# Hybrid trunk kernel: the gated branch and the residual stream turned by 16-bit DMA transposes through one joint tile

## Chip, cores and metric

The kernel runs on one core of a Trainium2 chip. The metric is the device time of one execution in microseconds (us), as the median of the runs. Lines are those of the kernel before (L120 is line 120), unless the text says that they are of the changed kernel.

## What is computed

Four layers on a residual stream x of 256 tokens by 2048 channels, all float32. Each layer normalizes x, multiplies it with one wide input projection, runs a mixer (layers 0 and 3: chunked spatial gating, gMLP; layer 1: forgetting attention; layer 2: differential attention) beside a four-head attention to 256 memory tokens, gates the 2048 joined channels and adds an output projection to x:

```python
for i in range(DEPTH):
    h = rms_norm(x, norm_g[i])
    z = h @ w_in
    ...
    mq = rms_norm(mem_q.reshape(B, S, MEM_HEADS, HEAD_DIM), mem_q_norm_g[i])
    mem_out = memory_attention(mq, mk, mv)
    branch = jnp.concatenate([mix_out, mem_out], axis=-1) * jax.nn.silu(gate)
    x = x + branch @ w_out[i]
```

## The kernel before

**Products and slots.** All large products have tokens on the output partitions: two accumulators of 128 tokens by 512 columns (`acc[0]`, `acc[1]`) form a chunk. The weights arrive as 592 pieces of 256 rows by 512 columns, laid out as a 128x1024 tile (`raw`, 512 KB). A piece makes one slot: 12 TensorE matmuls of 512 columns (L186 to L188). Float32 is kept by splitting each operand into two rounded parts, hi and lo: ScalarE copies `raw` to `whi` (L119), VectorE subtracts to `wlo` (L120), and the three products hi\*hi, hi\*lo, lo\*hi are summed. Eight slots make a chunk.

**What sets the order.** The program is written out in order for TensorE, ScalarE, VectorE and SyncE; each engine keeps the order in which Python reaches its instructions. Ahead of each slot `between_slots` (L144) first lets every running task go on to its next `yield` (`tick`), then splits the piece that is three slots ahead (`split_until`, four buffers each for `whi` and `wlo`), then issues the load of a piece seven slots ahead, then runs the functions put on `late`. I call the work that an engine is given ahead of slot n its stage n. So work that a task gives to an engine in one stage stands ahead of that stage's split, and the split of stage n is needed by TensorE three slots later. ScalarE's split waits until TensorE has left slot n - 1, which frees the buffer.

**Turned tiles.** The next product contracts over channels, so results with tokens on partitions must be turned to have channels there. Three tasks do this:

- `norm_task` (L357) for queries and keys: it normalizes an accumulator (`qn`, L350), separates the upper and lower 16-bit halves of each tile on ScalarE (`pl`, L373), has SyncE issue a DMA transpose of the 16-bit tile (`tt`, L375), and one slot later does the same for the second 128 tokens. Three slots after that VectorE puts the halves together (`qt_t`, L382), ScalarE scales them into `qt`, `kt`, `mqt` or `mkt` (L386), and in the same stage `done()` sets the flag that starts the attention.
- `gate_task` (L632), 16 times: silu of the gate's accumulator (`sg`), times the mixer's output (`br`, L644); then in each of the next two slots TensorE transposes four 128x128 blocks into PSUM (L653), from which `bh` (L657, L659) and `bl` (L663, L665) are made, the operand of the output projection.
- `residual_task` (L813), 12 times with a turn (layers 0 to 2, four chunks each): the new x (`xn`, L827), its store, its squares (L836, put on `late`), and in each of the next two slots four TensorE transposes (L846) and a split into `xh` and `xl` (L221, L222), the operand of the next layer's input projection.

The output projection takes its operand parts in the order 0, 1, 2, 3, 6, 7, 4, 5 in its first chunk (L93), because parts 4 and 5 come from the last gate.

**Memory attention.** `memory` (L870) spawns the memory query's `norm_task` and an `attention_task` (L575) that waits for its flag. That task has 8 units, one per slot: scores of unit n on TensorE (L501), exponential on ScalarE (L509), transposes of the probabilities two slots on (L602), their product with the values three slots on (L593).

Of the kernel before, what the change touches and what calls it, by code (L numbers as in the profile page):

```python
# [20 lines left out]
P = 128  # L21
# [3 lines left out]
KT = D // P  # L25
# [18 lines left out]
def trunk_kernel(  # L44
# [251 lines left out]
    def token_rms(src, r):  # L296
        ss = small.tile([P, 2, 4], F32, tag="ss", name="ss", bufs=2)
        rows = {}
        for n in range(6):
            if n >= 2:  # L300
                for t, row in enumerate(rows.pop(n - 2)):
                    nc.scalar.activation(
                        row, row, AF.Square, accum_out=ss[:, t, n - 2 : n - 1]
                    )
            if n < 4:
                rows[n] = []
                for t in range(2):
                    row = tmp.tile([P, CW], F32, tag="tb", name="row", bufs=4)
                    nc.sync.dma_start(
                        row, src[t * P : (t + 1) * P, n * CW : (n + 1) * CW]  # L310
                    )
                    rows[n].append(row)
            if n < 5:
                yield
        late.append(lambda: finish_rms(ss, r))

    def square_rows(src, rcols):
        sqs = []
        for t in range(2):
            sq = tmp.tile([P, CW], F32, tag="sq", name="sq", bufs=2)  # L320
            if rcols is None:
                nc.scalar.activation(sq, src[t], AF.Square)
            else:
                nc.scalar.activation(sq, src[t], AF.Square, scale=rcols[:, t : t + 1])
            sqs.append(sq)
        return sqs
# [21 lines left out]
    def times_cols(dst, src, cols, n):  # L348
# [5 lines left out]
            ALU.mult,  # L354
        )

    def norm_task(acc, rcols, gain, width, dst, done=None):  # L357
        sqs = square_rows(acc, rcols)
        sc = []
        late.append(lambda: sc.extend(norm_factors(sqs, rcols, width)))  # L360
        yield
        yield
        yield
        qn = []
        for t in range(2):
            q = tmp.tile([P, CW], F32, tag="tb", name="qn", bufs=4)
            times_cols(q, acc[t], sc[t], CW // width)
            qn.append(q)
        turned = []
        for t in range(2):  # L370
            pl = tmp.tile([P, 2, CW], U16, tag="pl", name="pl", bufs=2)
            halves = qn[t].bitcast(U16).rearrange("p (e h) -> p h e", h=2)
            nc.scalar.copy(pl, halves)  # L373
            tt = tmp.tile([P, 8, P], U16, tag="tt", name="tt", bufs=2)
            nc.sync.dma_start_transpose(tt, pl.rearrange("p h e -> p (h e)"))  # L375
            turned.append(tt)
            yield
        yield
        yield
        for t in range(2):  # L380
            qt = tmp.tile([P, CW], F32, tag="tb", name="qt_t", bufs=4)
            nc.vector.tensor_copy(  # L382
                qt.bitcast(U16).rearrange("p (c r h) -> p h c r", c=4, h=2),
                turned[t].rearrange("p (h c) r -> p h c r", h=2),
            )
            nc.scalar.activation(  # L386
                dst[:, :, t * P : (t + 1) * P], qt.rearrange("p (c r) -> p c r", c=4),
                AF.Copy, scale=gain,
            )
        if done:  # L390
            done()

# [70 lines left out]

    def diff_setup():
        ls = small.tile([P, 8], F32, tag="sc", name="lsum")
        pr = tmp.tile([P, CW], F32, tag="sq", name="pr", bufs=2)
# [11 lines left out]
        wrow = tmp.tile([P, CW], F32, tag="sq", name="wrow", bufs=2)  # L478
# [153 lines left out]
    def gate_task(acc, rcols, mos, c, dst, pscale):  # L632
        sgs = []
        for t in range(2):
            sg = tmp.tile([P, CW], F32, tag="ta", name="sg", bufs=2)
            nc.scalar.activation(sg, acc[t], AF.Silu, scale=rcols[:, t : t + 1])
            sgs.append(sg)
        yield
        while mos[c] is None:
            yield  # L640
        br = []
        for t in range(2):
            b = tmp.tile([P, CW], F32, tag="tb", name="br", bufs=4)
            nc.vector.tensor_mul(b, mos[c][t], sgs[t])  # L644
            br.append(b)
        for j in range(2):
            yield
            kp = 2 * c + j
            tb = ps_t.tile([P, 4, P], F32, tag="t", name="tb")
            for kk in range(2):  # L650
                for t in range(2):
                    f = (2 * j + kk) * P
                    nc.tensor.transpose(tb[:, 2 * kk + t, :], br[t][:, f : f + P], ident)  # L653
            tbf = tb.rearrange("p a b -> p (a b)")
            hi, lo = new_parts("b", kp)
            if pscale is None:
                nc.scalar.copy(hi, tbf)  # L657
            else:
                nc.scalar.activation(hi, tbf, AF.Copy, scale=pscale)  # L659

            def rest(hi=hi, lo=lo, tbf=tbf):
                if pscale is None:
                    nc.vector.tensor_sub(lo, tbf, hi.bitcast(F32))  # L663
                else:
                    nc.vector.scalar_tensor_tensor(  # L665
                        lo, tbf, pscale, hi.bitcast(F32), ALU.mult, ALU.subtract
                    )

            late.append(rest)
            dst[kp] = (hi, lo)  # L670


    def gmlp_norm_task(vs, j, flag):
# [139 lines left out]
    def residual_task(acc, i, n, xo, ss, r_next):  # L813
        last = i == DEPTH - 1
        xn = []
        for t in range(2):
            rows, cols = slice(t * P, (t + 1) * P), slice(n * CW, (n + 1) * CW)
            xt = tmp.tile([P, CW], F32, tag="tb", name="xn", bufs=4)
            if last:
                for a in (0, CW // 2):  # L820
                    w = slice(a, a + CW // 2)
                    nc.vector.tensor_add(xt[:, w], acc[t][:, w], xo[t][:, w])
                    (nc.sync, nc.scalar)[a > 0].dma_start(
                        out[rows, cols.start + w.start : cols.start + w.stop], xt[:, w]
                    )
                continue
            nc.vector.tensor_add(xt, acc[t], xo[t])  # L827
            nc.gpsimd.dma_start(x_d[i][n][t], xt)  # L828
            xn.append(xt)
        if last:  # L830
            return

        def squares():
            for t in range(2):
                sq = tmp.tile([P, CW], F32, tag="sq", name="sq", bufs=2)
                nc.scalar.activation(sq, xn[t], AF.Square, accum_out=ss[:, t, n : n + 1])  # L836

        late.append(squares)
        for jj in range(2):
            yield  # L840
            kp = 2 * n + jj
            tb = ps_t.tile([P, 4, P], F32, tag="t", name="tb")
            for kk in range(2):
                for t in range(2):
                    f = (2 * jj + kk) * P
                    nc.tensor.transpose(tb[:, 2 * kk + t, :], xn[t][:, f : f + P], ident)  # L846
            hi, lo = new_parts("x", kp)
            scaled_split(hi, lo, tb.rearrange("p a b -> p (a b)"), KT * (i + 1) + 2 * kp)
            xparts[kp] = (hi, lo)
        if n == 3:  # L850
            finish_rms(ss, r_next)

# [210 lines left out]
```

## Time and profile before

| | |
|---|---|
| median of 3 runs | 1774.13 us (1773.99 to 1775.26) |
| profiled execution, its own time | 1775.19 us |
| its span, first to last instruction | 1773.2 us |
| busy: TensorE matmul, weight load | 1756.5 us, 1445.6 us |
| busy: VectorE, ScalarE, GpSimd | 1045.2 us, 938.6 us, 115.6 us |
| mean granted TensorE clock | 0.999 |
| moved by DMA | 364.38 MB, mean 205 GB/s |

The profiled execution is 1.06 us above the median, and 2.0 us of it lie outside its span. Busy times of TensorE come from pipelined matmuls and overlap, so the distance from one matmul's start to the next one's says more than a busy share. In a timeline row the first two numbers are the start and the length in us; x4 at its end means four instructions merged; a bracket tells the engine's idle time just before it and what ended it.

### The profile page before, as it was taken

What the parts mean: (1) busy time and instruction counts of PE and PEld (TensorE: products, weight loads), DVE (VectorE), ACT (ScalarE), POOL (GpSimd) and SP (SyncE); (2) the same over time, 40 slices, a digit from 0 to 9 for tenths busy, and PEclk for the clock granted to TensorE, in tenths of its full rate; (3) what the DMA queues carried; (4) which work ended last, traced back from release to release, by engine and by line L of the source; (5) the groups of instructions that cost most, each with busy time, mean ns of one, the idle gap of its engine ahead of it and who ended that gap; (6) DMA issues with size and microseconds to landing.
All of it is one profiled execution on the core that took longest, in us unless ns stands there. A gap on an engine that the chain in (4) does not pass through costs nothing.

```text
span 1773.2 us, 22090 instructions
## 1 busy us (share of the span) xinstructions
PE 1756.5 (99%) x8142; PEld 1445.6 (82%) x8142; DVE 1045.2 (59%) x1479; ACT 938.6 (53%) x1313; POOL 115.6 (7%) x138
## 2 busy tenths in 40 slices
PE   9999999999999999999999999999999999999999
PEld 6788887888888878888888887878788888788887
DVE  5655667555555656656555566766665556655553
ACT  5656645544555655556445555665654554554532
POOL 1110101000001001011000110102000000100000
PEclk9999999999999999999999999999999999999999
DMA  8878865555676566566866656645546666545564
GB/s 295 291 240 279 267 229 166 179 183 184 224 232 203 177 209 185 171 201 186 207 224 230 210 179 199 185 163 190 187 159 224 231 218 221 178 165 179 190 219 161
DMA packets 146843, 364.38 MB, mean 205 GB/s; under 512 B 54396, under 2 KB 56756, under 8 KB 146608
## 3 DMA queue, kind: packets, MB, share of 16 engines
q1 hardware_dynamic: 140016, 343.33, 59.9%
q0 software_dynamic: 5280, 18.44, 3.3%
q8 instruction: 64, 1.05, 0.2%
q10 hardware_dynamic: 1440, 1.22, 0.2%
q14 instruction: 43, 0.35, 0.1%
HBM read 339.55 MB, written 12.89 MB: 199 GB/s over the span
## 4 chain that ended last, share of the span: by engine, by line
PE 92%; DMA 3%; issue 2%; ACT 2%; DVE 1%; POOL 0%; SPq 0%; ACTq 0%; DVEq 0%; POOLq 0%
PE acc L186 29%; PE acc L188 28%; PE acc L187 28%; PE tb L593 2%; PE tb L602 1%; PE tb L653 1%; DMA xraw<-in_mem_t_dram 1%; PE s L543 1%; PE s L501 1%; PE sv L719 1%; DMA tt<-pl 1%; PE tb L846 1%; ACT whi L119 1%; DMA bias<-cum_d 1%; DMA row<-in_mem_dram 0%
## 5 line engine op out<-in xcount | busy, mean ns | idle before, releaser
L120 DVE TENSOR_TENSOR wlo<-raw,whi 128x1024 fp32r<-128x1024 f32 x591 | 722.0, 1225 | 569.9 <-ACT whi L119 563.5
L119 ACT CAST whi<-raw 128x1024 fp32r<-128x1024 f32 x591 | 619.3, 1050 | 477.4 <-PE acc L188 400.6
L186 PE MATMUL acc<-whi,xh 128*128 128x512 f32 x1600 | 640.3, 400 | 0.0
L188 PE MATMUL acc<-whi,xl 128*128 128x512 f32 x1600 | 624.8, 390 | 0.0
L187 PE MATMUL acc<-wlo,xh 128*128 128x512 f32 x1600 | 624.2, 390 | 0.0
L186 PEld LDWEIGHTS acc<-whi,xh 128*128 128x128 f32 x1600 | 301.0, 188 | 66.3 <-issue 3.5
L188 PEld LDWEIGHTS acc<-whi,xl 128*128 128x128 f32 x1600 | 300.5, 188 | 64.2
L187 PEld LDWEIGHTS acc<-wlo,xh 128*128 128x128 f32 x1600 | 301.2, 188 | 59.0 <-DVE wlo L120 0.2
L186 PE MATMUL acc<-whi,bh 128*128 128x512 f32 x764 | 300.0, 393 | 0.7 <-ACT bh L221 0.4
L187 PE MATMUL acc<-wlo,bh 128*128 128x512 f32 x764 | 298.1, 390 | 1.2 <-DVE wlo L120 0.9
L188 PE MATMUL acc<-whi,bl 128*128 128x512 f32 x764 | 297.9, 390 | 0.2 <-DVE bl L222 0.2
L187 PEld LDWEIGHTS acc<-wlo,bh 128*128 128x128 f32 x764 | 143.5, 188 | 32.3 <-DVE wlo L120 2.9
L188 PEld LDWEIGHTS acc<-whi,bl 128*128 128x128 f32 x764 | 143.4, 188 | 30.7 <-DVE bl L222 0.5
L186 PEld LDWEIGHTS acc<-whi,bh 128*128 128x128 f32 x764 | 143.5, 188 | 30.6 <-ACT bh L221 0.8
L336 POOL TENSOR_TENSOR sc<-sc,expo 128x8 f32<-128x8 f32 (+1 forms) x23 | 56.6, 2460 | 512.6 <-DVE sc L335 450.3
L606 ACT COPY pt<-tb 128x256 f32<-128x256 f32 (+1 forms) x80 | 27.2, 339 | 114.0 <-PE tb L602 113.9
L373 ACT COPY pl<-qn 128x1024 uint16<-128x1024 uint16 x40 | 41.8, 1044 | 44.8 <-DVE qn L350 42.7
L657 ACT CAST bh<-tb 128x512 fp32r<-128x512 f32 x26 | 15.3, 587 | 48.0 <-PE tb L653 48.0
L222 DVE SCALAR_TENSOR_TENSOR xl<-tb,gk,xh 128x256 fp32r<-128x256 f32 x48 | 23.2, 484 | 29.4 <-ACT xh L221 29.3
L221 ACT ACTIVATE xh<-tb,gk 128x256 fp32r<-128x256 f32 x48 | 22.8, 475 | 32.8 <-PE tb L846 19.5
L828 POOL DMA_DIRECT2D x_d<-xn x24 | 13.2, 549 | 311.9 <-DVE xn L827 311.1
L506 DVE TENSOR_REDUCE st<-s 128x1 f32<-128x256 f32 x32 | 13.5, 421 | 31.5 <-PE s L501 31.5
(167 smaller groups left out, 972.6 us busy)
## 6 DMA issues: line engine op xcount, KB each, us to landing
raw<-in_w_a_dram SPq DMA_DIRECT2D x176, 512.0 KB, 3.3
raw<-in_w_o_dram SPq DMA_DIRECT2D x128, 512.0 KB, 3.9
raw<-in_w_b_dram SPq DMA_DIRECT2D x112, 512.0 KB, 3.5
raw<-in_w_c_dram SPq DMA_DIRECT2D x112, 512.0 KB, 3.3
raw<-in_w_kv_dram SPq DMA_DIRECT2D x63, 512.0 KB, 4.9
x_d<-xn POOLq DMA_DIRECT2D x24, 256.0 KB, 6.3
xo<-x_d SPq DMA_DIRECT2D x24, 256.0 KB, 5.5
lnp<-in_ln_dram SPq DMA_DIRECT2D x12, 256.0 KB, 5.6
```

Source lines behind the costliest of these rows:

```text
L119: nc.scalar.copy(hi, raw)
L120: nc.vector.tensor_sub(lo, raw, hi.bitcast(F32))
L186: nc.tensor.matmul(acc[t], xh[:, c], wh, start=begin, stop=False)
L187: nc.tensor.matmul(acc[t], xh[:, c], wl, start=False, stop=False)
L188: nc.tensor.matmul(acc[t], xl[:, c], wh, start=False, stop=end)
L221: nc.scalar.activation(hi, src, AF.Copy, scale=g)
L222: nc.vector.scalar_tensor_tensor(lo, src, g, hi.bitcast(F32), ALU.mult, ALU.subtract)
L336: nc.gpsimd.tensor_tensor(sc[:, :, :n], sc[:, :, :n], expo.rearrange("p (a b) -> p a b", a=2)[:, :, :n], ALU.pow,)
L373: nc.scalar.copy(pl, halves)
L501: nc.tensor.matmul(s[:, :S], qt[:, h, t * P : (t + 1) * P], mk[:, h * S : (h + 1) * S], start=True, stop=True,)
L593: nc.tensor.matmul(av, pt[:, j * P : (j + 1) * P], vv[:, j, f], start=(j == 0), stop=(j == tiles(t) - 1),)
L606: nc.scalar.copy(pt[:, : nk * P], tb[:, : nk * P])
```

## The change

Two helpers are new. `turn` separates the 16-bit halves of a 128x512 tile on ScalarE and has SyncE issue the DMA transpose; `join` puts two turned tiles (both token halves) together on VectorE into one tile `wide` (128 x 4 x 2 x 128, a single buffer). All three tasks now use them: both halves are turned in one stage, and joined two stages later. `gate_task` and `residual_task` no longer use TensorE; their hi and lo parts are made from `wide` in SBUF. The gate multiplies in place into the mixer's output tile. In `norm_task` one activation over the joint tile takes the place of two, and one more `yield` stands between it and `done()`. Buffers: `pl` now shares the tag of `sq` (3 buffers instead of 2), `tb` has 3 instead of 4, and the rows of `token_rms` move to the tag `mo`.

```diff
+    def turn(src):
+        pl = tmp.tile([P, CW], F32, tag="sq", name="pl", bufs=3).bitcast(U16)
+        nc.scalar.copy(
+            pl.rearrange("p (h e) -> p h e", h=2),
+            src.bitcast(U16).rearrange("p (e h) -> p h e", h=2),
+        )
+        tt = tmp.tile([P, 8, P], U16, tag="tt", name="tt", bufs=2)
+        nc.sync.dma_start_transpose(tt, pl)
+        return tt
+
+    def join(wide, tts):
+        for t in range(2):
+            nc.vector.tensor_copy(
+                wide[:, :, t, :].bitcast(U16).rearrange("p c (r h) -> p h c r", h=2),
+                tts[t].rearrange("p (h c) r -> p h c r", h=2),
+            )
+
+    def new_wide():
+        return tmp.tile([P, 4, 2, P], F32, tag="tw", name="wide", bufs=1)
...
     def norm_task(acc, rcols, gain, width, dst, done=None):
...
+        tts = [turn(q) for q in qn]
+        yield
+        yield
+        wide = new_wide()
+        join(wide, tts)
+        nc.scalar.activation(
+            dst.rearrange("p c (t r) -> p c t r", t=2), wide, AF.Copy, scale=gain
+        )
+        yield
         if done:
             done()
...
     def gate_task(acc, rcols, mos, c, dst, pscale):
...
-            nc.vector.tensor_mul(b, mos[c][t], sgs[t])
-            br.append(b)
+            nc.vector.tensor_mul(mos[c][t], mos[c][t], sgs[t])
+            tts.append(turn(mos[c][t]))
+        yield
+        yield
+        wide = new_wide()
+        join(wide, tts)
         for j in range(2):
-            yield
+            src = wide[:, 2 * j : 2 * j + 2].rearrange("p a b r -> p (a b r)")
             kp = 2 * c + j
-            tb = ps_t.tile([P, 4, P], F32, tag="t", name="tb")
-            for kk in range(2):
-                for t in range(2):
-                    f = (2 * j + kk) * P
-                    nc.tensor.transpose(tb[:, 2 * kk + t, :], br[t][:, f : f + P], ident)
...
             dst[kp] = (hi, lo)
+            yield
...
     def residual_task(acc, i, n, xo, ss, r_next):
...
         late.append(squares)
+        tts = [turn(xt) for xt in xn]
+        yield
+        yield
+        wide = new_wide()
+        join(wide, tts)
         for jj in range(2):
-            yield
             kp = 2 * n + jj
-            tb = ps_t.tile([P, 4, P], F32, tag="t", name="tb")
-            for kk in range(2):
-                for t in range(2):
-                    f = (2 * jj + kk) * P
-                    nc.tensor.transpose(tb[:, 2 * kk + t, :], xn[t][:, f : f + P], ident)
...
             xparts[kp] = (hi, lo)
+            yield
```

**ScalarE, layer 0, around the first chunk of the new x.** `pl` is the tile of separated halves, `sq` the squares, `xh` the hi part of the new operand. Before:

```order
L119 CAST whi<-raw 128x1024 x6
L836 ACTIVATE sq,ss<-xn 128x512 x2
L221 ACTIVATE xh_3895<-tb,gk 128x256 x2
L119 CAST whi<-raw 128x1024
L221 ACTIVATE xh_3924<-tb,gk 128x256 x2
L119 CAST whi<-raw 128x1024 x7
```

Now (lines of the changed kernel):

```order
L360 COPY pl<-xn 128x1024 x2
L119 CAST whi<-raw 128x1024
L843 ACTIVATE sq,ss<-xn 128x512 x2
L119 CAST whi<-raw 128x1024
L221 ACTIVATE xh_3905<-wide,gk 128x256 x2
L119 CAST whi<-raw 128x1024
L221 ACTIVATE xh_3929<-wide,gk 128x256 x2
L119 CAST whi<-raw 128x1024 x5
```

Two copies stand ahead of the split of the chunk's first stage, and the first `xh` comes two stages after them instead of one.

**VectorE, layer 1, the memory query's norm.** `wlo` is the split of a stage, `qt_t` and `wide` the joining of turned halves, `st<-s` the first look at the attention's scores. Before:

```order
L350 TENSOR_TENSOR qn<-acc_4412,sc 128x512
L350 TENSOR_TENSOR qn<-acc_4413,sc 128x512
L120 TENSOR_TENSOR wlo<-raw,whi 128x1024 x4
L382 COPY qt_t<-tt 128x2x512 x2
L506 TENSOR_REDUCE st<-s 128x1
```

Now:

```order
L350 TENSOR_TENSOR qn<-acc_4409,sc 128x512
L350 TENSOR_TENSOR qn<-acc_4410,sc 128x512
L120 TENSOR_TENSOR wlo<-raw,whi 128x1024 x2
L370 COPY wide<-tt 128x2x4x128 x2
L120 TENSOR_TENSOR wlo<-raw,whi 128x1024
L515 TENSOR_REDUCE st<-s 128x1
```

The joining stands two splits after `qn` instead of four, and the scores one split after the joining; against `qn`, the scores come one stage earlier than before.

**SyncE, the first keys of the start, one piece of the difference.** `raw` are the loads of weight pieces.

```order
-L375 DMA_TRANSPOSE tt<-pl 128x8x128
-L106 DMA raw<-in_w_kv_dram 128x1024
-L375 DMA_TRANSPOSE tt<-pl 128x8x128
-L106 DMA raw<-in_w_kv_dram 128x1024 x15
-L375 DMA_TRANSPOSE tt<-pl 128x8x128
-L106 DMA raw<-in_w_kv_dram 128x1024
-L375 DMA_TRANSPOSE tt<-pl 128x8x128
-L106 DMA raw<-in_w_kv_dram 128x1024 x4
+L365 DMA_TRANSPOSE tt<-pl 128x8x128 x2
+L106 DMA raw<-in_w_kv_dram 128x1024 x16
+L365 DMA_TRANSPOSE tt<-pl 128x8x128 x2
+L106 DMA raw<-in_w_kv_dram 128x1024 x5
```

The two transposes of a pair are now issued back to back, ahead of the load of their stage.

## Rows read from the trace of the kernel before

**Rows 1.** The page: busy time and share of TensorE, and its granted clock in 40 slices.

```profile
PE 1756.5 (99%) x8142; PEld 1445.6 (82%) x8142; DVE 1045.2 (59%) x1479; ACT 938.6 (53%) x1313; POOL 115.6 (7%) x138
...
PEclk9999999999999999999999999999999999999999
```

**Rows 2.** The page: the chain that ended last, shares of the span by engine.

```profile
PE 92%; DMA 3%; issue 2%; ACT 2%; DVE 1%; POOL 0%; SPq 0%; ACTq 0%; DVEq 0%; POOLq 0%
```

**Rows 3.** Timeline of TensorE, output projection of layer 0, 495 to 505 us.

```profile
495.26 0.39 PE L188 MATMUL acc<-whi,bl 128*128 128x512 f32 x1
...
495.49 0.60 PE L846 MATMUL tb<-ident,xn 128*128 128x128 f32 x4
...
497.09 0.39 PE L188 MATMUL acc<-whi,bl 128*128 128x512 f32 x1
...
501.67 0.39 PE L188 MATMUL acc<-whi,bl 128*128 128x512 f32 x1
...
503.03 0.39 PE L188 MATMUL acc<-whi,bl 128*128 128x512 f32 x1
```

**Rows 4.** Groups by line: busy us, mean ns of one | idle before, releaser.

```profile
L120 DVE TENSOR_TENSOR wlo<-raw,whi 128x1024 fp32r<-128x1024 f32 x591 | 722.0, 1225 | 569.9 <-ACT whi L119 563.5 <-DMA xraw<-in_mem_t_dram 2.6 <-DMA row<-in_x_dram 2.5
L119 ACT CAST whi<-raw 128x1024 fp32r<-128x1024 f32 x591 | 619.3, 1050 | 477.4 <-PE acc L188 400.6 <-issue 33.2 <-ACT whi L119 9.4
L373 ACT COPY pl<-qn 128x1024 uint16<-128x1024 uint16 x40 | 41.8, 1044 | 44.8 <-DVE qn L350 42.7 <-DMA raw<-in_w_b_dram 2.1
L382 DVE COPY qt_t<-tt 128x1024 uint16<-128x1024 uint16 x40 | 28.0, 744 | 1.9 <-DMA tt<-pl 1.9
L221 ACT ACTIVATE xh<-tb,gk 128x256 fp32r<-128x256 f32 x48 | 22.8, 475 | 32.8 <-PE tb L846 19.5 <-DVE xl L222 13.3
L653 PE MATMUL tb<-ident,br 128*128 128x128 f32 x128 | 19.3, 273 | 0.0
L846 PE MATMUL tb<-ident,xn 128*128 128x128 f32 x96 | 14.4, 272 | 0.0
```

**Rows 5.** The tile `tt`: its issues (ns min/median/max), and time to landing.

```profile
L375 SPq DMA_TRANSPOSE tt<-pl x40: 1237/1237/1331, 65.5 to 1521.3; - x40
...
DMA to landing us min/median/max: 2.7/4.3/6.9
```

**Rows 6.** Waits of TensorE: us in total, times, longest us.

```profile
PE s L501 <- ACT mqt L386: 4.6, 4, 1.2
PE sv L719 <- ACT p L509: 3.9, 2, 2.3
```

**Rows 7.** Timelines of ScalarE, VectorE, TensorE: memory query's norm, layer 0, 266 to 312 us.

```profile
281.37 1.05 ACT L373 COPY pl<-qn 128x1024 uint16<-128x1024 uint16 x1 [3.72 <-DVE qn L350]
...
284.54 0.54 DVE L695 TENSOR_SCALAR v<-v,mv 128x512 f32<-128x512 f32 x1
...
285.85 0.69 DVE L699 TENSOR_TENSOR v<-v,lnp 128x512 f32<-128x512 f32 x1
...
291.40 0.70 PE L501 MATMUL s<-mk,mqt 128*128 128x256 f32 x2 [1.24 <-ACT mqt L386]
```

**Rows 8.** Timelines of SyncE's queue and TensorE: the same norm in layer 1.

```profile
570.76 1.25 SPq L375 DMA_TRANSPOSE tt<-pl  x1
...
581.25 0.70 PE L501 MATMUL s<-mk,mqt 128*128 128x256 f32 x2 [1.13 <-ACT mqt L386]
```

**Rows 9.** Timelines of VectorE and ScalarE: first new x of layer 0, 468 to 500 us.

```profile
469.78 1.28 DVE L827 TENSOR_TENSOR xn<-acc,xo 128x512 f32<-128x512 f32 x2
...
470.27 1.06 ACT L119 CAST whi<-raw 128x1024 fp32r<-128x1024 f32 x1 [1.67 <-PE acc L188]
...
471.22 0.63 ACT L836 ACTIVATE sq<-xn 128x512 f32<-128x512 f32 x1
```

**Rows 10.** Busy time by stretch: us, engines' busy us (instructions), granted clock, DMA share, GB/s.

```profile
301.60:305.00 3.40, 3.40 (x12) 2.82 (x11) 2.33 (x6) 0.98 (x3) 0.00 (x0) 0.50 0.54 180
```

**Rows 11.** The page: what DMA moved in the whole span.

```profile
DMA packets 146843, 364.38 MB, mean 205 GB/s; under 512 B 54396, under 2 KB 56756, under 8 KB 146608
```

More of the change, by code (lines that the diff above doesn't have):

```diff
@@ L307, in token_rms @@
                 for t in range(2):
-                    row = tmp.tile([P, CW], F32, tag="tb", name="row", bufs=4)
+                    row = tmp.tile([P, CW], F32, tag="mo", name="row", bufs=6)
                     nc.sync.dma_start(
@@ L319, in square_rows @@
         for t in range(2):
-            sq = tmp.tile([P, CW], F32, tag="sq", name="sq", bufs=2)
+            sq = tmp.tile([P, CW], F32, tag="sq", name="sq", bufs=3)
             if rcols is None:
@@ L365, in norm_task @@
         for t in range(2):
-            q = tmp.tile([P, CW], F32, tag="tb", name="qn", bufs=4)
+            q = tmp.tile([P, CW], F32, tag="tb", name="qn", bufs=3)
             times_cols(q, acc[t], sc[t], CW // width)
             qn.append(q)
-        turned = []
-        for t in range(2):
[L371 to L376, printed above, removed]
-            yield
+        tts = [turn(q) for q in qn]
         yield
         yield
-        for t in range(2):
[L381 to L389, printed above, removed]
+        wide = new_wide()
[4 more added lines that the diff above has]
+        yield
         if done:
@@ L465, in diff_setup @@
         ls = small.tile([P, 8], F32, tag="sc", name="lsum")
-        pr = tmp.tile([P, CW], F32, tag="sq", name="pr", bufs=2)
+        pr = tmp.tile([P, CW], F32, tag="sq", name="pr", bufs=3)
         for m in range(2):
@@ L477, in diff_setup @@
         nc.tensor.matmul(pb[:NH, :384], rel, onehot, start=True, stop=True)
-        wrow = tmp.tile([P, CW], F32, tag="sq", name="wrow", bufs=2)
+        wrow = tmp.tile([P, CW], F32, tag="sq", name="wrow", bufs=3)
         nc.vector.tensor_copy(wrow[:NH, :384], pb[:NH, :384])
@@ L640, in gate_task, with rest @@
             yield
-        br = []
+        tts = []
         for t in range(2):
-            b = tmp.tile([P, CW], F32, tag="tb", name="br", bufs=4)
-            nc.vector.tensor_mul(b, mos[c][t], sgs[t])
-            br.append(b)
+            nc.vector.tensor_mul(mos[c][t], mos[c][t], sgs[t])
[4 more added lines that the diff above has]
+        join(wide, tts)
         for j in range(2):
-            yield
+            src = wide[:, 2 * j : 2 * j + 2].rearrange("p a b r -> p (a b r)")
             kp = 2 * c + j
-            tb = ps_t.tile([P, 4, P], F32, tag="t", name="tb")
-            for kk in range(2):
-                for t in range(2):
-                    f = (2 * j + kk) * P
-                    nc.tensor.transpose(tb[:, 2 * kk + t, :], br[t][:, f : f + P], ident)
-            tbf = tb.rearrange("p a b -> p (a b)")
             hi, lo = new_parts("b", kp)
             if pscale is None:
-                nc.scalar.copy(hi, tbf)
+                nc.scalar.copy(hi, src)
             else:
-                nc.scalar.activation(hi, tbf, AF.Copy, scale=pscale)
-            def rest(hi=hi, lo=lo, tbf=tbf):
+                nc.scalar.activation(hi, src, AF.Copy, scale=pscale)
+            def rest(hi=hi, lo=lo, src=src):
                 if pscale is None:
-                    nc.vector.tensor_sub(lo, tbf, hi.bitcast(F32))
+                    nc.vector.tensor_sub(lo, src, hi.bitcast(F32))
                 else:
                     nc.vector.scalar_tensor_tensor(
-                        lo, tbf, pscale, hi.bitcast(F32), ALU.mult, ALU.subtract
+                        lo, src, pscale, hi.bitcast(F32), ALU.mult, ALU.subtract
                     )
@@ L817, in residual_task @@
             rows, cols = slice(t * P, (t + 1) * P), slice(n * CW, (n + 1) * CW)
-            xt = tmp.tile([P, CW], F32, tag="tb", name="xn", bufs=4)
+            xt = tmp.tile([P, CW], F32, tag="tb", name="xn", bufs=3)
             if last:
@@ L834, in squares @@
             for t in range(2):
-                sq = tmp.tile([P, CW], F32, tag="sq", name="sq", bufs=2)
+                sq = tmp.tile([P, CW], F32, tag="sq", name="sq", bufs=3)
                 nc.scalar.activation(sq, xn[t], AF.Square, accum_out=ss[:, t, n : n + 1])
         late.append(squares)
-        for jj in range(2):
-            yield
-            kp = 2 * n + jj
-            tb = ps_t.tile([P, 4, P], F32, tag="t", name="tb")
-            for kk in range(2):
-                for t in range(2):
-                    f = (2 * jj + kk) * P
-                    nc.tensor.transpose(tb[:, 2 * kk + t, :], xn[t][:, f : f + P], ident)
-            hi, lo = new_parts("x", kp)
-            scaled_split(hi, lo, tb.rearrange("p a b -> p (a b)"), KT * (i + 1) + 2 * kp)
-            xparts[kp] = (hi, lo)
+        tts = [turn(xt) for xt in xn]
[3 more added lines that the diff above has]
+        join(wide, tts)
+        for jj in range(2):
+            kp = 2 * n + jj
+            hi, lo = new_parts("x", kp)
+            scaled_split(
+                hi, lo, wide[:, 2 * jj : 2 * jj + 2].rearrange("p a b r -> p (a b r)"),
+                KT * (i + 1) + 2 * kp,
+            )
+            xparts[kp] = (hi, lo)
+            yield
         if n == 3:
```

## The prediction

> **What bounds the kernel now.** I read the page first, for which engine is full and at which clock: TensorE is busy 99% of the span, at full clock in every slice, VectorE 59% and ScalarE 53% [rows 1]. Then the chain that ended last: 92% of it is TensorE [rows 2]. So almost every instruction that leaves TensorE's queue shortens the span, and the other engines matter only where TensorE waits for them. Third, TensorE's timeline, for what a transpose really costs there. From 501.67 to 503.03 us six matmuls start in 1.36 us, 0.227 us each; a slot of twelve is 2.72 us. From 495.26 to 497.09 there are also six steps, with four transposes among them, and they take 1.83 us. Four transposes cost 0.47 us [rows 3]. Fourth, TensorE's waits: the list is short. Its largest entries are 4.6 us for the memory query `mqt` (once per layer) and 3.9 us for an exponential in the two gMLP layers [rows 6].
>
> **What is removed.** 16 gates and 12 residual chunks, each with two groups of four transposes: 56 groups, the 128 and 96 transposes of [rows 4]. 56 x 0.47 = **26.3 us**. Lower bound: the merged row of four is 0.60 us long and one is 0.27, so starts lie (0.60 - 0.27) / 3 = 0.11 us apart, 0.44 for four [rows 3, 4], 24.6 us in all. A row's own length, 273 ns, is no price, since the next one starts after 0.11 us. The Trainium skill (TensorE: Matmul & The Clock Gate, Part 4: PE-mode transpose) gives about 275 ns for a 128x128 transpose inside a kernel, at two bytes; the row's length agrees. Priced so, 224 transposes would be 61.6 us and the forecast some 35 us lower; the distance of the starts decides against it.
>
> **What is added off TensorE.** 56 tiles (16 x 2 and 12 x 2) are turned as `norm_task`'s 40 are today. Each costs ScalarE a copy of 1.04 us and VectorE a joining of 0.74 us [rows 4]: 58 us on an engine idle for 835 us, 42 us on one idle for 728 [rows 1]. In `norm_task` one activation replaces two, so ScalarE gains a little. The hi and lo parts are as many as before. The tiles are 256 KB: 56 x 0.26 = 14.7 MB on 364 MB [rows 11], 4% more traffic. SyncE gets 56 issues of 1.24 us [rows 5]; queued behind them are the loads of weight pieces, issued four slots before their split, so about 2.5 us of delay is covered.
>
> **Does the supply of weights hold?** The pair is now joined two stages after it was turned, and VectorE and ScalarE stop there if it has not landed. I follow the first residual chunk [rows 9]. The adds begin at 469.78 and take 0.64 each; the copies run 470.4 to 472.5; the split of that stage 473.5; squares to 474.9; the next split on ScalarE 475.9, on VectorE 477.1 (1.05 and 1.22 [rows 4]). The first transpose is issued at 471.5, the second 1.24 later, at 472.7. It lands L later; today's 40 took 2.7 to 6.9 us, median 4.3 [rows 5]. Behind the landing come a joining (0.74), two `xh` (0.95), the stage's split on ScalarE (1.05) and on VectorE (1.22): 476.7 + L. TensorE needs that split in the fifth slot after 470.25, at 484.1 with its first lo product. So TensorE is served as long as **L is under 7.4 us**. At L = 5 the margin is 2.4 us, at the largest L of today 0.5. A gate's chain is of the same kind (one cast for the two `xh`); its parts 4 and 5 are first read six and seven slots after the gate's product, and are made in stages 3 and 4. The new x has its parts 6 and 7 in stages 2 and 3 and is read in slots 6 and 7. I put the cost at nothing; the cover is the three slots of split weights.
>
> **The memory query.** Here TensorE does stand behind the turned tile. Counted from the end of its product, the query was turned in stages 3 and 4, joined in 7 and read by TensorE in slot 7. Now: turned in 3, joined in 5, read in slot 6. The extra `yield` gives a stage, but the scores also come one slot sooner.
> - Layer 0 [rows 7]: copies 281.37 to 283.5, second issue 283.7, split 284.5 and 285.75, then the gMLP norm's three operations (1.92 us), split to 288.9, joinings 289.65 and 290.4, one activation (about 1.1, as the 1024-element copy of [rows 4] takes 1.04): `mqt` at 291.5, or 292.5 at L = 6.9. Slot 7's scores were due at 291.40 - 1.24 = 290.16, so slot 6's at 287.44. Wait 4.1 to 5.1 us. Layer 3 has the same order of work: the same.
> - Layer 1 [rows 8]: issues 570.76 and 572.0; the second lands at 576.3 (L = 4.3) to 578.9; VectorE is free at 575.3. `mqt` at 578.2 to 580.8, wanted at 581.25 - 1.13 - 2.72 = 577.4. Wait 0.8 to 3.4 us; I take 1.3 (L a little above today's median, since two share the engines). Layer 2 likewise.
>
> Together 10.8 us (9.8 to 17.0) for 4.6 today: **+6.2 us** (+5.2 to +12.4). That the flag is set "later" saves nothing by itself.
>
> **Next waits.** The gMLP layers' 3.9 us [rows 6] come from ScalarE's table loads piling up behind a late `mqt`. With TensorE held one slot earlier the exponentials regain some of that: I take **-2.5 us** (0 to -3.9). Behind the wait in layer 0 the granted clock was 0.50, the lower of its two levels (1.2 of 2.4 GHz), for 3.4 us [rows 10], a loss of 1.7; it may go, or come in layer 3 too: 0 (-1.7 to +1.7). In layers 1 and 2 the memory attention still runs when the next query is joined, and ScalarE's stop there delays a copy of probabilities by up to 2 us, twice: **+1 us** (0 to +4).
>
> **Sum.** -26.3 + 6.2 - 2.5 + 0 + 1 = -21.6. The profiled execution took 1775.19 us and would take 1753.6; it was 1.06 above the median of the runs, so I say **1752.5 us**. With all bounds one way: -26.7 (1747.4) and -6.5 (1767.6).
>
> **Rivals.**
> 1. *The turned tiles come too late: slower.* If two transposes issued back to back take L over 7.4 us in the output projection, beside the loads of the old and the stores of the new x, TensorE runs out of split weights in each of the 28 gate and residual pairs: 1752.5 + 28 x (L - 7.4). Break-even lies at L = 8.2; slower by over 0.2% from L = 8.3; at L = 9 it is 1797 us. For it: the largest of today's is 6.9, and each had the queue to itself. Against it: the median is 4.3 and the whole change is 4% of traffic. The Trainium skill (VectorE: DVE Perf Modes, The three transpose paths and Rules for kernel authors) says to use TensorE where a PSUM destination will do, with 390 ns for a 128x128 two-byte block there and 1309 ns by DMA. Eight such blocks in a row, as one tile has, would be an estimate of 10.5 us and this rival; the trace lands a whole tile in 4.3, so I hold to the row.
> 2. *The gain is handed back by halves.* L between 7.6 and 8.2 on average, or joinings that cost twice 0.74 us through their new access pattern: 1758 to 1775, typically 1769.
> 3. *The query's wait vanishes.* If VectorE reached the joining earlier than I think, all of 4.6, 3.9 and 1.7 us would go: 1775.2 - 26.3 - 10.2 - 1.1 = 1738. Against it: in layer 0 VectorE's own queue holds the joining until 288.9, after slot 6 is due, whatever L is.
>
> That the change might not do what it says I leave out: in the program's order all 56 groups are gone.
>
> **How the numbers follow.** A measurement of this kernel tells a change from none at about 0.2%, 3.5 us. Forecast 0.75 (1747.4 to 1767.6, all of it faster). Rival 1: 0.10 (0.07 slower, 0.03 same). Rival 2: 0.09 (0.04 faster, 0.05 same). Rival 3: 0.06, faster. So faster 0.85, same 0.08, slower 0.07. The range 1745 to 1768 holds the forecast's bounds and leaves out rival 1, half of rival 2 and rival 3, 0.2 in all.
>
> **What would show it.** In the changed profile TensorE's queue should hold transposes of probabilities alone, and matmuls of a residual chunk should start 0.227 us apart throughout. `tt` should show 96 landings with a median of 4 to 6 us; over 7.4 is rival 1, with waits of TensorE for `wlo` or `whi` after a joining. The waits for `mqt` should be about 4 us in layers 0 and 3 and 1 to 2 us in 1 and 2; near zero would be rival 3. If the time falls by 26 us or more with those waits present, the price of a transpose was too low; if transposes are gone and the time stays, look for the new waits in the output projections.

## The result, and the profile after

The changed kernel takes **1757.74 us** (median of 4 runs, 1757.08 to 1759.51) where the kernel before took 1774.16 (4 runs). The ratio is 0.9908 with a 95% interval of 0.9891 to 0.9925: 16.4 us faster, inside the range, where 21.6 were forecast. A later run (run 5 below) whose instructions stood in exactly the same order on every engine gave 0.9892 (0.9877 to 0.9907), so a difference of 2 us between two runs below is not told by the time alone; the waits in the traces tell more.

The profiled execution took 1757.08 us, 18.1 less than that of before. The page of the changed kernel, beside [rows 1] and [rows 11]:

```profile
PE 1736.1 (99%) x7918; PEld 1428.6 (81%) x7918; DVE 1073.9 (61%) x1535; ACT 982.7 (56%) x1349; POOL 122.3 (7%) x138
...
PEclk9999999999999999999999999999999999999999
...
DMA packets 205980, 379.06 MB, mean 216 GB/s; under 512 B 113532, under 2 KB 115892, under 8 KB 205744
...
L370 DVE COPY wide<-tt 128x1024 uint16<-128x1024 uint16 x96 | 68.8, 747 | 20.1 <-DMA tt<-pl 19.5
```

TensorE has 224 instructions fewer (8142 to 7918) and is still full; 14.7 MB more move, as counted ahead. A joining takes 0.747 us (0.744 before). New is the idle time in the last row: VectorE stands 19.5 us for tiles that have not landed (1.9 in [rows 4]).

TensorE's waits, the whole span, beside [rows 6]; then the memory query's wait alone in stretches of layers 0, 1, 2 and 3:

```profile
PE s L510 <- ACT mqt L395: 7.3, 4, 3.7
PE acc L186 <- ACT whi L119: 3.1, 2, 2.8
PE acc L187 <- DVE wlo L120: 2.3, 3, 0.8
...
PE s L510 <- ACT mqt L395: 3.7, 1, 3.7
...
PE s L510 <- ACT mqt L395: 0.2, 1, 0.2
...
PE s L510 <- ACT mqt L395: 0.2, 1, 0.2
...
PE s L510 <- ACT mqt L395: 3.3, 1, 3.3
```

Three things are to be seen. `mqt` costs 7.3 us where 4.6 stood, all but 0.4 of it in layers 0 and 3. The wait of `sv` for an exponential (3.9) is gone. And TensorE now waits for split weights, 5.4 us in all (`wlo` 0.9 before). That last one the prediction had put at nothing.

The granted clock, in stretches that answer to [rows 10] (columns as there):

```profile
290.30:294.00 3.70, 3.23 (x8) 2.56 (x9) 2.31 (x3) 3.67 (x5) 0.00 (x0) 0.54 0.26 66
...
853.70:857.20 3.50, 3.50 (x10) 2.74 (x9) 3.47 (x4) 1.35 (x3) 0.00 (x0) 0.51 0.79 263
...
1509.10:1515.90 6.80, 5.58 (x13) 4.43 (x14) 2.85 (x4) 4.88 (x6) 0.00 (x0) 0.50 0.49 158
```

Three stretches lie near the lower of the two levels (0.50 is 1.2 of 2.4 GHz) where there was one, each behind a standstill of TensorE: for `mqt`, for split weights, for `mqt` again. In 0.5 and 1.2 us of the first and the third TensorE still stood for `mqt`, which the waits count already. What the clock costs is the busy time times what is missing: 3.23 x 0.46 + 3.50 x 0.49 + 5.58 x 0.50 = 6.0 us, against 1.7 before.

The turned tile, beside [rows 5]:

```profile
L365 SPq DMA_TRANSPOSE tt<-pl x96: 1232/1293/8426, 65.6 to 1669.9; - x96
...
DMA to landing us min/median/max: 2.7/3.6/11.0
```

The median landing is shorter than before (3.6 for 4.3; 4 to 6 were forecast). But one issue held SyncE's queue 8.4 us, and one landing took 11.0, far over the 7.4 that the prediction allowed. They belong to one pair, the issue to its second transpose and the landing to its first. It is the first gate of layer 1 (timelines of GpSimd, SyncE's queue, VectorE and TensorE):

```profile
828.41 4.42 POOL L505 DMA_DIRECT2D bias<-bias_d  x8 [39.53 <-DVE lg L532]
...
837.04 9.87 SPq L365 DMA_TRANSPOSE tt<-pl  x2
...
848.05 0.75 DVE L370 COPY wide<-tt 128x1024 uint16<-128x1024 uint16 x1 [6.49 <-DMA tt<-pl]
848.96 0.74 DVE L370 COPY wide<-tt 128x1024 uint16<-128x1024 uint16 x1 [0.16 <-DMA tt<-pl]
...
851.35 0.50 PE L186 MATMUL acc<-whi,xh 128*128 128x512 f32 x1 [2.75 <-ACT whi L119]
852.61 0.51 PE L187 MATMUL acc<-wlo,xh 128*128 128x512 f32 x1 [0.76 <-DVE wlo L120]
```

GpSimd has started to load layer 2's bias at 828.41, as soon as layer 1's attention had read the old one. Two transposes are issued into that transfer: 9.87 us for both instead of some 2.6. VectorE stands 6.49 us at the joining, and TensorE 2.75 + 0.76 = 3.5 us behind it. The prediction's sum counts L from the second issue. That one ended at 846.91 and took 8.43, so it began at 838.48; its tile was there at 848.96, so L is 10.5 and the sum gives 10.5 - 7.4 = 3.1, 0.4 less than measured.

The other 1.9 us of weight waits lie in layer 2. ScalarE's timeline, the first key there:

```profile
1126.91 1.05 ACT L360 COPY pl<-qn 128x1024 uint16<-128x1024 uint16 x1 [0.89 <-DVE qn L350]
1131.83 1.05 ACT L360 COPY pl<-qn 128x1024 uint16<-128x1024 uint16 x1 [3.88 <-DMA tt<-pl]
```

The second rearranging copy waits 3.88 us for the landing of the first transpose. `pl` took over the tag of `sq`, with three buffers for four users here (two squares of the differential attention, two `pl`), so it gets the buffer that this transpose is still reading.

### The profile page after: what moved, and what is told of

It is laid out like the page before. It is cut to its first block, busy times and chain, and to the rows that moved or that the text cites. A ratio compares the mean times of both kernels' runs of the same rounds, so it can differ in the third digit from the quotient of the medians.

```text
span 1755.3 us, 21797 instructions
## 1 busy us (share of the span) xinstructions
PE 1736.1 (99%) x7918; PEld 1428.6 (81%) x7918; DVE 1073.9 (61%) x1535; ACT 982.7 (56%) x1349; POOL 122.3 (7%) x138
## 4 chain that ended last, share of the span: by engine, by line
PE 91%; DVE 3%; DMA 3%; ACT 2%; issue 1%; SPq 0%; ACTq 0%; DVEq 0%
PE acc L186 29%; PE acc L187 28%; PE acc L188 28%; PE tb L602 2%; DVE wlo L120 1%; DMA xraw<-in_mem_t_dram 1%; DMA tt<-pl 1%; PE s L510 1%; ACT whi L119 1%; PE tb L611 1%; PE s L552 1%; PE sv L726 1%; DVE wide L370 0%; PE s L527 0%; DMA raw<-in_w_kv_dram 0%
## 5 line engine op out<-in xcount | busy, mean ns | idle before, releaser
L119 ACT CAST whi<-raw 128x1024 fp32r<-128x1024 f32 x591 | 612.7, 1048 | 332.1 <-PE acc L188 239.9
L370 DVE COPY wide<-tt 128x1024 uint16<-128x1024 uint16 x96 | 68.8, 747 | 20.1 <-DMA tt<-pl 19.5
L221 ACT ACTIVATE xh<-wide,gk 128x256 fp32r<-128x256 f32 x48 | 21.8, 501 | 44.0 <-DVE wide L370 44.0
L360 ACT COPY pl<-mo 128x1024 uint16<-128x1024 uint16 x32 | 31.9, 1043 | 23.8 <-DVE mo L652 23.8
L663 ACT CAST bh<-wide 128x512 fp32r<-128x512 f32 x26 | 16.1, 617 | 44.0 <-DVE wide L370 44.0
L360 ACT COPY pl<-xn 128x1024 uint16<-128x1024 uint16 x24 | 23.9, 1044 | 22.7 <-DVE xn L834 22.7
```

The costliest lines, as they stand in the source:

```text
L119: nc.scalar.copy(hi, raw)
L221: nc.scalar.activation(hi, src, AF.Copy, scale=g)
L360: nc.scalar.copy(pl.rearrange("p (h e) -> p h e", h=2), src.bitcast(U16).rearrange("p (e h) -> p h e", h=2),)
L370: nc.vector.tensor_copy(wide[:, :, t, :].bitcast(U16).rearrange("p c (r h) -> p h c r", h=2), tts[t].rearrange("p (h c) r -> p h c r", h=2),)
```

## The experiments

The edits are against the changed kernel. Ratios are to the kernel before on the same chip; "the change" stands for its two measurements, 1757.7 and 1755.7 us.

**1. A fourth buffer.**

```
-            sq = tmp.tile([P, CW], F32, tag="sq", name="sq", bufs=3)
+            sq = tmp.tile([P, CW], F32, tag="sq", name="sq", bufs=4)
...                                   # the same for pl, pr and wrow
-            q = tmp.tile([P, CW], F32, tag="tb", name="qn", bufs=3)
+            q = tmp.tile([P, CW], F32, tag="tb", name="qn", bufs=2)
...                                   # the same for xn
```

> The tag of the squares and of the rearranged tiles gets a fourth buffer (and the tag of xn and qn two in place of three, so that it fits). Theory (shared buffer): in layer 2 the second rearranging copy of a key or query waits for the first transpose's landing because its buffer is the one that this transpose reads; with a fourth buffer the copy at 1131.8 and the one at 1208.7 start with no wait for tt (3.9 and 4.1 us now), and the stalls of TensorE at 1141 and 1212 to 1219 us (about 2.9 us together) go: 1754 to 1756. Rival (slow landings): the landing itself is late, the tile then waits in the next step; TensorE's stalls stay at the same places: 1757 to 1758.

1754.99 us, ratio 0.9895 (0.9882 to 0.9909), span 1753.4 for 1755.3. ScalarE in the same place:

```profile
1129.11 2.00 ACT L360 COPY pl<-qn 128x1024 uint16<-128x1024 uint16 x2 [0.89 <-DVE qn L350]
```

The second copy runs right behind the first, and TensorE has no wait at all between 1120 and 1230 us, where it had 1.9 (not the 2.9 that were expected). The time alone would not tell this from a repetition; span and waits agree on 1.9 us. The shared buffer was the cause; the landing did not become the next wait.

**2. The first gate of layer 1 behind the bias.**

```
         while mos[c] is None:
             yield
+        for _ in range(pause):        # 5 for layer 1, gate 0; otherwise 0
+            yield
```

> The first gate of layer 1 multiplies and turns its product five slots (13.6 us) later; its parts are wanted more than 16 slots later. Theory (collision): the second transpose's 8.4 us issue at 837 us comes from the transfer of layer 2's bias, in flight from 828 to about 843; moved behind it the issue takes 1.3 to 3.5 us, TensorE's stall of 4 us at 848 to 853 and the half clock behind it go: 1751.5 to 1754. Rival (a pair of transposes is slow wherever it stands): the long issue moves along with the gate and the stall appears 13 us later, 1757 to 1758.

1752.00 us, ratio 0.9878 (0.9863 to 0.9893). SyncE's queue, the same pair of transposes, and what is left of TensorE's waits from 840 to 880 us:

```profile
853.26 2.92 SPq L365 DMA_TRANSPOSE tt<-pl  x2
```

```profile
PE acc L187 <- DVE wlo L120: 0.9, 2, 0.8
```

Stretches (columns as in [rows 10]), first in the change during the long issue, then here:

```profile
840.00:842.00 2.00, 2.00 (x10) 1.65 (x10) 1.57 (x3) 0.00 (x0) 0.00 (x0) 1.00 1.07 121
...
853.00:857.00 4.00, 4.00 (x20) 3.30 (x19) 1.83 (x2) 4.00 (x6) 0.00 (x0) 1.00 1.09 241
```

The pair takes 2.92 us where it took 9.87, in the whole kernel the longest landing is now 7.3, and the stretch from 853 to 857 us runs at a granted clock of 1.00. So the pair is not slow wherever it stands; five slots later it is quick. The gain is 3.7 to 5.7 us; the 2.6 of the waits and the 1.7 of the clock make 4.3. That the bias transfer holds the issue rests on the time alone, since the pair was moved and not the bias; which resource of it does so was not tried. The share of the DMA engines doesn't tell: it is 1.07 in the change, with 121 GB/s moved, and 1.09 here, with 241.

**3. The flag one slot later still**, so that scores stand in slot 7 as in the kernel before.

```
         yield
+        if pause:                     # memory query only
+            yield
         if done:
             done()
```

> The memory attention's flag is set one slot later, so that the scores stand in slot 7 as in the kernel before; nothing else moves. Theory (the query's wait is bought by the earlier slot): the wait for mqt falls from 7.3 us to about 2 (3.7 to 1 in layers 0 and 3), and with it the half clock at 290 and 1509 us, 1.7 to 5 us; the gMLP layers' wait for an exponential may come back in part (0 to 3.9): 1748 to 1755, most likely 1751. Rival (what is saved at mqt is paid at the exponential, slot for slot): 1757 to 1758 with 3 to 4 us of waits of sv for p.

1756.07 us, ratio 0.9904 (0.9890 to 0.9917): the rival's value. TensorE's waits:

```profile
PE sv L728 <- ACT p L520: 5.6, 2, 2.8
...
PE s L512 <- ACT mqt L395: 1.6, 2, 1.0
```

Of the 7.3 us for `mqt` 1.6 are left, and 5.6 stand at `sv`. The two waits are one: 7.3 in the change, 7.2 here. When scores are asked for later, the exponential comes behind them too late for the gMLP's mixing. The half clock moved along too (0.64 from 303 to 306.5 us and 0.71 from 1519 to 1523, behind the two waits). My likeliest value, 1751, is refuted.

**4. The norms alone**, with `gate_task` and `residual_task` as in the kernel before.

> Only the change to the norms (one joint tile, flag one slot later); gates and residual rows are turned by TensorE as in the kernel before. Theory: the whole gain is the 56 groups of transposes; the norms alone cost the longer wait for mqt (+2.7), more half clock (0 to 3) and the stall at 1131 to 1219 us (up to +3), and save the gMLP layers' exponential wait (-3.9): 1773 to 1778, about the time of the kernel before. Rival (the joint tile of the norms brings part of the gain and the gates and residual rows give half of theirs back): 1764 to 1768.

1776.00 us for 1773.19, ratio 1.0010 (1.0002 to 1.0019): no gain. The first wait is the same as in the change, and there is none for an exponential:

```profile
PE s L510 <- ACT mqt L395: 7.3, 4, 3.7
PE acc L187 <- DVE wlo L120: 1.9, 3, 0.8
```

All of the gain comes from the 56 groups of transposes.

**5. The query's task ahead of the gMLP norm's** in the list of tasks of layers 0 and 3 (a `spawn` that puts it first).

> In the gMLP layers (0 and 3) the memory query's task runs ahead of the gMLP norm's in each stage, so that VectorE joins the turned query before the norm's three operations (1.92 us) and not behind them; the flag stays where the change put it. In the changed kernel the second transpose lands at 286.4 us and the joining starts at 288.2. Theory (VectorE's queue sets mqt in these layers): mqt comes 1.8 us earlier, its wait falls from 3.7 to about 1.9 in both layers, no wait of sv takes its place since ScalarE is released earlier too; the half clock behind it may go as well (1.7 us each time): 1750 to 1754.5. Rival (ScalarE's chain of table load and exponential sets the time, as when the flag was set later): wait moves to sv, 1757 to 1758.

1755.68 us, ratio 0.9892 (0.9877 to 0.9907), the wait for `mqt` 7.4 us. The edit missed its aim: the norm's operations come every second stage, and that is the stage before the joining, not the same one. The instructions stood as in the change, on every engine. It serves as the second measurement.

**6. Fourth buffer, later gate and query first together.**

> Fourth buffer, first gate of layer 1 five slots later, and the query's task first in layers 0 and 3, together. If the three stalls are independent their gains add: -2.75 and -5.7 as measured one by one, and -3.5 for the query (estimate, 1.8 twice): 1745 to 1748. If one of them only moved a stall that the next one uncovers, 1749 to 1752.

1750.23 us, ratio 0.9862 (0.9849 to 0.9876). The number lies in the range given for a stall that only moves. But the third part is empty, and runs 1 and 2 alone, against the change's two measurements, add up to 4.4 to 8.5 us; 5.5 to 7.5 were found. TensorE's waits for split weights are 2.7 us here, 5.4 in the change. So the first two gains add up.

**7 and 8. Gates, then residual rows, turned by TensorE again**, the other tasks as in the change.

> The gates' products are turned by TensorE again, as before; norms and residual rows as in the change. Theory: 32 groups of four transposes at 0.47 us return (+15.0), the stall at 848 to 853 us and the half clock behind it go (-5.7, as the run with the later gate showed): 1766 to 1768.5. Rival (the gates gained little on TensorE since their transposes filled waits): 1753 to 1760.

> The residual rows are turned by TensorE again, as before; norms and gates as in the change. Theory: 24 groups at 0.47 us return (+11.3), nothing else changes since no wait of TensorE stands behind a turned residual tile now: 1768 to 1770. Rival (pairs of transposes beside loads and stores of x cost TensorE time that the waits don't show): 1758 to 1765.

1765.96 us, ratio 0.9948 (0.9935 to 0.9960), and 1768.16 us, 0.9961 (0.9948 to 0.9973). Without turned gates there is no stall at 848 us: from 835 to 880 TensorE waits for nothing. So 32 groups cost 8.2 to 10.3 us by the times, and with the stall and the half clock behind it (3.5 + 1.7) 13.4 to 15.5, 0.42 to 0.48 each; 24 groups cost 10.4 to 12.5 us, 0.43 to 0.52 each. The starts in the traces settle it more closely. Measured as in [rows 3], from the matmul ahead of a group to the sixth one behind it, a group of run 7 adds 0.46 us in the mean (0.35 to 0.59), one of run 8 also 0.46 (0.45 to 0.47). Together that is 14.7 + 11.1 = **25.8 us**, where 56 x 0.47 = 26.3 were summed. The Trainium skill's 275 ns for a transpose (TensorE: Matmul & The Clock Gate, Part 4: PE-mode transpose) would make 32 groups an estimated 35.2 us and 24 groups 26.4: as a price in a full queue it is more than twice too much here.

**9. The gMLP norm one stage later, and the query first**, what run 5 had meant to do.

```
+        yield
         for t in range(2):            # gmlp_norm_task
             stats = small.tile(...)
```

> The run with the query's task first left the order of the instructions on every engine as it was, since the gMLP norm's operations stand in the stage before the joining and not in the same one. Here the norm's steps also start one stage later, so that on VectorE the query's product is scaled ahead of one triple of the norm's operations and joined ahead of the next. Theory (VectorE's queue sets mqt in layers 0 and 3): scaling comes 1.9 us earlier and with it the transposes, the joining waits for the landing alone, and mqt comes about 3.4 us earlier; its wait falls from 3.7 to under 1 in both layers: 6 to 7 us less than the change (1755.7 to 1757.7 in two measurements), a few more if the half clock behind the wait goes: 1747 to 1751.5. Rival (the sum of mqt's and the exponentials' waits is set by ScalarE's table loads, as with the later flag): sv waits for p by 5 to 6 us instead, 1755 to 1758.

1748.27 us, ratio 0.9859 (0.9846 to 0.9872). Layer 0 in the change, VectorE (a triple of the norm begins, the joining) and TensorE (the scores):

```profile
285.14 0.54 DVE L702 TENSOR_SCALAR v<-v,mv 128x512 f32<-128x512 f32 x1
...
288.19 1.35 DVE L370 COPY wide<-tt 128x1024 uint16<-128x1024 uint16 x2
...
290.77 1.22 PE L510 MATMUL s<-mk,mqt 128*128 128x256 f32 x2 [3.68 <-ACT mqt L395]
```

Here, the query's scaling, one triple of the norm, the joining, the next triple, and the scores; then TensorE's waits in the whole span and a stretch with its clock:

```profile
280.34 1.28 DVE L354 TENSOR_TENSOR qn<-acc,sc 128x512 f32<-128x512 f32 x2
281.54 0.53 DVE L707 TENSOR_SCALAR v<-v,mv 128x512 f32<-128x512 f32 x1
...
286.31 1.38 DVE L374 COPY wide<-tt 128x1024 uint16<-128x1024 uint16 x2
287.57 0.54 DVE L707 TENSOR_SCALAR v<-v,mv 128x512 f32<-128x512 f32 x1
...
288.93 0.70 PE L514 MATMUL s<-mk,mqt 128*128 128x256 f32 x2 [1.11 <-ACT mqt L399]
```

```profile
PE s L514 <- ACT mqt L399: 2.5, 4, 1.1
...
289.00:294.00 5.00, 5.00 (x22) 4.17 (x23) 4.24 (x7) 4.97 (x8) 0.00 (x0) 1.00 0.51 166
```

7.3 us become 2.5 (1.1 in each of the two layers, where under 1 was expected), no `sv` appears in the list, and from 289 to 294 us and from 1503 to 1508 the granted clock is 1.00. The wait did not move to the exponential, since here ScalarE is released earlier instead of TensorE later: 4.8 us of waits and up to 4.3 of clock, 7.4 to 9.5 measured. So VectorE's queue set `mqt` in these layers.

**10. Runs 6 and 9 together.**

> The combination of before (fourth buffer, first gate of layer 1 later: 1750.2) with the shifted norm. If VectorE's queue sets mqt: 1741 to 1745. If the wait only moves to the exponentials: 1749 to 1751.

**1743.01 us**, ratio 0.9827 (0.9812 to 0.9842), 30.2 us faster than before and 12.7 to 14.7 faster than the change. The three causes add up.

**11 and 12. The joining one stage earlier, and one later**, for gates and residual rows.

```
         tts.append(turn(...))         # gate_task; the same in residual_task
         yield
-        yield                         # 11: earlier
+        yield                         # 12: later (a third one)
         wide = new_wide()
```

> Gates and residual rows are joined one stage after they were turned, in place of two. By the prediction's sum TensorE is then served only as long as the second transpose lands within 4.7 us of its issue (7.4 less a slot of 2.72). The landings are 2.7 to 11.0 us, median 3.6, with issues that last up to 3.4 us in the residual chunks: theory (the margin is real): 0 to 0.5 us lost in each of 28 pairs, 0 to 14, and 2.7 more in the stall at 848 us: 1760 to 1772, with waits of TensorE for whi and wlo all over the output projections. Rival (the supply has more slack than the sum counted): only the stall at 848 us grows: 1757 to 1760.

1787.44 us, ratio 1.0075 (1.0059 to 1.0091): 30 us behind the change, and slower than the kernel before. The direction is the theory's, but the size is beyond its 1772. TensorE's waits; the first residual chunk on SyncE's queue, VectorE and TensorE; three stretches with their clock:

```profile
PE acc L186 <- ACT whi L119: 12.7, 10, 5.2
PE acc L187 <- DVE wlo L120: 11.7, 16, 0.8
```

```profile
469.65 4.80 SPq L365 DMA_TRANSPOSE tt<-pl  x2
...
475.64 1.65 DVE L370 COPY wide<-tt 128x1024 uint16<-128x1024 uint16 x2 [2.86 <-DMA tt<-pl]
...
479.22 0.51 PE L186 MATMUL acc<-whi,bh 128*128 128x512 f32 x1 [0.80 <-ACT whi L119]
480.48 0.50 PE L187 MATMUL acc<-wlo,bh 128*128 128x512 f32 x1 [0.75 <-DVE wlo L120]
...
479.00:484.00 5.00, 4.03 (x10) 2.97 (x11) 4.80 (x6) 3.81 (x6) 0.00 (x0) 0.71 0.54 183
...
861.00:865.00 4.00, 3.33 (x7) 2.35 (x8) 3.82 (x5) 3.52 (x5) 0.00 (x0) 0.50 0.36 124
...
978.00:983.00 5.00, 5.00 (x13) 3.88 (x12) 3.15 (x3) 2.23 (x3) 0.00 (x0) 0.52 0.83 250
```

The profiled execution is the longest of the six (1790.55 us, the shortest 1781.89) and 33.5 us behind the change's. Its weight waits are 24.4 us where the change has 5.4. Each standstill also costs more than its row: the matmul with 0.80 starts 1.19 us after the one ahead of it (478.03), where 0.227 is usual, so 0.96 are lost. Counted by such distances of starts, waits cost 24.6 us more than in the change, and the half clock 5.8 more (mean clock 0.991 for 0.996; over all runs 0.991 to 0.995 for 0.995 to 0.997). That is 30.4 of 33.5; the other 3 us are not placed. The formula missed both that a tile late for `whi` is late for `wlo` too (0.80 and 0.75 here), and the half clock after it.

> The counterpart of the joining one stage earlier: gates and residual rows are joined three stages after they were turned, in place of two; nothing else differs from the change. By the sum TensorE is then served up to a landing of 7.4 + 2.72 = 10.1 us, so of the stall at 848 us (3.5 us with a landing of 11.0) some 0.8 is left and the half clock behind it goes: 4.4 us less than the change's 1755.7 to 1757.7, 1751 to 1754. All other pairs were in time already and give nothing. Rival (parts of the new x or of the next gate are then made too late for their own slots): waits of TensorE for bh, xh or bl, 1757 or more.

1751.57 us, ratio 0.9870 (0.9854 to 0.9887). TensorE's waits between 840 and 870 us:

```profile
PE acc L187 <- DVE wlo L120: 0.8, 1, 0.8
```

The landings there are still 11.0 and, from the second issue, 10.4 us, but of 3.5 us of waits 0.8 are left, and 848 to 856 us run at a granted clock of 1.00. The expectation's 0.8 came from the first landing; with the second the sum gives 10.4 - 10.1 = 0.3, so it is short by some 0.5, as in the change. The gain is 4.1 to 6.2 us, 4.4 forecast. Runs 11 and 12 point the same way on either side of the change: stages between turning and joining decide how late a tile may land.

## Why the prediction was nearly right

Both sides in the profiled executions, in us:

| term | forecast | found | shown by |
|---|---|---|---|
| 56 groups of transposes | -26.3 | -25.8 | starts in runs 7 and 8; run 4 |
| `mqt` | +6.2 | +2.7 | waits after, [rows 6] |
| exponential before `sv` | -2.5 | -3.9 | waits after |
| half clock | 0 (-1.7 to +1.7) | +4.3 | stretches after, [rows 10] |
| supply of split weights | 0 | +4.5 | runs 1, 2, 12 |
| joinings that hold up probabilities | +1 | no such wait listed | waits after |
| sum | -21.6 | -18.2 | measured: -18.1 |

**The bound and the price of a transpose held.** TensorE's queue was the limit, and the distance of starts, not the row's length, is what a transpose costs there. The rule of the Trainium skill that spoke against the change (VectorE: DVE Perf Modes, Rules for kernel authors: TensorE where a PSUM destination will do) is not borne out here: with the same tiles on TensorE runs 7 and 8 took 8.2 to 10.3 and 10.4 to 12.5 us longer than the change, and a whole tile of 128x512 lands in 3.6 us in the median.

**The memory query: mechanism right, size off.** In layer 0 the wait behind VectorE's queue was forecast at 4.1 to 5.1 us and measured 3.7 (3.3 in layer 3); run 9 shows that the queue is indeed the cause. In layers 1 and 2 I took 1.3 us from a landing a little above the median of 4.3; it came within 3.5 us in layer 1, and 0.2 us were left. My "rival 3" (the wait vanishes) failed for the reason given, yet moving the norm brought most of it about (2.5 of 7.3 us left).

**The step that failed is "I put the cost at nothing".** The formula L < 7.4 held to half a microsecond: the one second transpose that broke it, L = 10.5, cost 3.5 us where it gives 3.1, and run 12, with a slot more, left 0.8 where it gives 0.3. What was wrong is the L that I fed it. I took 2.7 to 6.9 us from transposes of before, which were never issued beside the bias load, and did not go through what GpSimd's queue has in flight when each new pair is issued. The trace of before had it, eight loads from 839.34 us on:

```profile
839.34 4.43 POOL L496 DMA_DIRECT2D bias<-bias_d  x8 [39.52 <-DVE lg L523]
```

Second, the trouble in layer 2 does not come from L at all. The diff puts `pl` on the tag of `sq`, and I had listed no users of that tag; two squares and two halves in the same task need four.

**The half clock was under-priced.** I allowed 1.7 us either way. It follows waits: three standstills, three stretches, +4.3 us. Not each is followed by it: in run 4 the query's wait in layer 3 is 3.3 us long as in the change, and 1526 to 1534 us ran at 1.00. So it belongs in the range rather than the sum, at 0 to some 3 us for each standstill of 3 us.

The sum of the errors is small (3.4 us) because `mqt` (3.5 too much), the exponentials and the joinings (2.4) stand against clock, supply and the price of a transpose (9.3 too little). That 5.9 and 9.3 us nearly cancel is luck; what was not luck is the 25.8 us of transposes.

## What to carry to other kernels

When work moves from a full engine to a DMA queue, work out how late its result may land and then look, place by place, at what other queues have in flight there; one slot of slack was worth 30 us on one side (run 11) and 4 to 6 on the other (run 12). A buffer tag that takes on a new user is to be counted task by task, as an engine's queue is. And a wait for a late operand is removed at its source: asking for it later only moved it (run 3), making room ahead of it on the engine that its tile waits for cut it from 7.3 to 2.5 us and removed the slow clock behind it (run 9).

## What was not expected of the hardware

An issue of a 16-bit transpose held SyncE's queue 1.24 us when it stood alone, but 8.4 us beside the bias transfer, with all loads of weights queued behind it. The pair in that place took 9.87 us, and 2.92 five slots later (run 2). In the twelve residual chunks, with the new x being stored, a pair took 4.5 to 5.0 us without TensorE waiting in the change (run 11's timeline shows the price when the slack is gone). Run 11 also shows that short standstills can have a second price: behind two of 0.80 and 0.75 us the mean granted clock from 479 to 484 us was 0.71, and in that whole execution, with 24.4 us of weight waits instead of 5.4, it was 0.991 for 0.996.
